# Low weight parts from ScalarE and an accumulating DMA instead of a VectorE subtraction, in a two-layer encoder trunk

## The chip, the cores and the metric

One core of one Trainium2 chip runs the whole program. The metric is the device time of one launch in microseconds. TensorE (PE) multiplies, VectorE (DVE) and ScalarE (ACT) work on 128 partitions, GpSimd (POOL) does a few small things, and SyncE (SP) issues the transfers from memory.

## The reference

Two layers of an encoder on 512 positions of width 1024, all in float32. A layer is a half-step feed-forward block (FFN), a mixer and a second half-step FFN:

```
h = x + 0.5 * swiglu(rms_norm(x, g1), w_gate, w_up, w_down)
z = rms_norm(h, g2) @ w_in            # u, v, xm, og
h = h + concat(spatial_gating(u, v), mlstm_mixer(xm, og)) @ w_out
x = h + 0.5 * swiglu(rms_norm(h, g3), w_gate, w_up, w_down)
```

The hidden width of an FFN is 2816. A final RMSNorm follows the second layer. Nearly all the arithmetic is in the products with the weights.

## The kernel before

Each product of float32 matrices is made of three matmuls on numbers that are rounded to a shorter format: weight and activation are each split into a high part (the rounded value) and a low part (the value less its high part), and high times high, high times low and low times high are added up in PSUM. A weight block is 128 x 1024 numbers (512 KB; 128 x 768 in the last down-projections of an FFN). One block is called a unit here, and a unit is used by 24 matmuls (18 for the small ones).

What a unit needs before PE can use it: an SP load into `raw` or `rawx`, an ACT copy into the high part `whi` or `whix`, and a DVE subtraction `raw - hi` into the low part `wlo` or `wlox`. Buffers set how far ahead this goes. `raw`, `whi` and `wlo` have three buffers each. Inside an FFN there are three more `rawx` and two more `whix` and `wlox`; the units of the gate and up product (the method `halves`) take `whix`/`wlox` and `whi`/`wlo` in turn. The down product and the mixer (the method `unit`) use `whi`/`wlo` alone. A unit's copy waits until PE is done with the unit that had the buffer.

The gate and up product of an FFN goes by pairs of hidden blocks, 43 pairs in all outside the very first, which is written out by hand. A pair has four weight blocks b11, b12, b22, b21 and uses seven units, e0 to e6 (`pair_plan`): e0, e3 and e5 are the plain blocks b11, b22 and b21; e1, e2, e4 and e6 are differences that `combine` makes on DVE in place. So e1 overwrites b11 with b12 - b11, and e6 overwrites b21. As seven is odd, the pairs alternate: in one e0 has the buffers `whi`/`wlo` and e3 and e5 have `whix`/`wlox`, in the next e0 has `whix`/`wlox`. On PE the seven units go into the PSUM banks pa, pe, pb, pe, pb, pa, pb in this order. An FFN has three groups of 4, 4 and 3 pairs, each followed by 8 down units; the last FFN of all runs its last 8 down units in two halves of the positions (`last_down`), with matmuls of half the width.

The program is put in order by a scheduler when it is built; on each engine the order is then fixed, and an instruction that waits holds up all that stand behind it. `load_params` makes small constants of the mixer on POOL at the start of each layer, from a transfer of parameters. POOL also adds up squares for the norms (`acc<-acc,sq`) and spreads rows in the mixer (`mb<-mr`).

Of the kernel before, what the change touches and what calls it, by code (L numbers as in the profile page):

```python
# [8 lines left out]
F32 = mybir.dt.float32  # L9
# [3 lines left out]
ALU = mybir.AluOpType  # L13
# [21 lines left out]
class Net:  # L35
# [77 lines left out]

    def unit(self, src, width=P):
        u = self.open_unit(src)
        self.fill(u, 0, u[0].shape[1])
        return self.views(u, width)

    def take(self):
# [12 lines left out]
        self.nc.sync.dma_start(out=raw, in_=src.rearrange("p j i c -> p (j i c)"))  # L132
        return raw

    def halves(self, raw):
        nc = self.nc
        self.wturn = getattr(self, "wturn", 0) + 1
        if self.wturn % 2:
            hi = self.phase.tile([P, 1024], F32R, tag="whix", name="whix", bufs=2)
            lo = self.phase.tile([P, 1024], F32R, tag="wlox", name="wlox", bufs=2)  # L140
        else:
            hi = self.wp.tile([P, 1024], F32R, tag="whi", name="whi")
            lo = self.wp.tile([P, 1024], F32R, tag="wlo", name="wlo")
        self.copied = nc.scalar.copy(hi, raw)  # L144
        nc.vector.tensor_tensor(out=lo, in0=raw, in1=hi.bitcast(F32), op=ALU.subtract)  # L145
        return tuple(t.rearrange("p (j i c) -> p j i c", j=4, i=2) for t in (hi, lo))

    def combine(self, out, a, c):
# [346 lines left out]
def pair_plan(blocks):  # L495
    st = {}

    def e0(b):
        st["b11"] = b.load(blocks[0])
        return b.halves(st["b11"])  # L500

    def e1(b):
        st["b12"] = b.load(blocks[1])
        b.combine(st["b11"], st["b12"], st["b11"])
        return b.halves(st["b11"])

    def e2(b):
        st["b22"] = b.load(blocks[2])
        b.combine(st["b11"], st["b22"], st["b11"])
        return b.halves(st["b11"])  # L510

    def e3(b):
        return b.halves(st["b22"])

    def e4(b):
        b.combine(st["b12"], st["b22"], st["b12"])
        return b.halves(st["b12"])

    def e5(b):
        st["b21"] = b.load(blocks[3])  # L520
        return b.halves(st["b21"])

    def e6(b):
        b.combine(st["b21"], st["b21"], st["b11"])
        return b.halves(st["b21"])

    return [e0, e1, e2, e3, e4, e5, e6]


# [631 lines left out]
```

## Time and profile before

| | |
|---|---|
| time, median of 3 runs | 1799.95 us (1799.25 to 1801.56) |
| time of the profiled execution | 1800.38 us |
| its span (first to last instruction) | 1798.7 us |
| PE busy | 1758.3 us (98%) |
| DVE busy | 1409.4 us (78%) |
| ACT busy | 880.4 us (49%) |
| POOL busy | 141.4 us (8%) |
| transfers from memory | 169.67 MB, the 16 DMA engines busy 31.0% of the span |
| granted TensorE clock, mean | 0.988 |

The profiled execution takes 1.7 us more than its span. Busy shares are means over stages that differ, so what an engine's relief is worth is read where PE waits.

### The profile page before, as it was taken

How to read it: one execution, taken by the hardware profiler on the slowest of the kernel's cores; microseconds unless marked ns; L12 is line 12 of the kernel's file. 1: busy time of each engine (PE TensorE's matmuls, PEld its weight loads, DVE VectorE, ACT ScalarE, POOL GpSimd, SP SyncE). 2: the span in 40 equal slices, each digit the busy share in tenths (PEclk: the TensorE clock that was granted, in tenths of full speed). 3: DMA queues.
4: the chain of work that ended last, by engine and by line, in shares of the span. 5: the costliest groups of instructions: out<-in, count | busy, mean ns of one | idle time of the engine just before them, and what ended most of it. 6: DMA issues, size and time to landing. Idle time of an engine off the chain costs nothing.

```text
span 1798.7 us, 28298 instructions
## 1 busy us (share of the span) xinstructions
PE 1758.3 (98%) x11602; PEld 1607.3 (89%) x11602; DVE 1409.4 (78%) x2062; ACT 880.4 (49%) x1233; POOL 141.4 (8%) x185
## 2 busy tenths in 40 slices
PE   8999999999998999999989999999999989999998
PEld 8989989887887989989889899898888889899898
DVE  8957958668988957958899587595698989597685
ACT  7434424457556534525565244344575555253255
POOL 5100000103012000000140000002030300000000
PEclk9999999999999999999999999999999989999999
DMA  5342422321241333323324233223122223233223
GB/s 187 94 130 94 128 73 80 99 80 50 69 140 48 110 125 94 119 82 100 99 69 141 83 94 122 91 73 105 59 60 83 94 83 126 86 105 118 83 77 109
DMA packets 51394, 173.60 MB, mean 97 GB/s; under 512 B 5824, under 2 KB 7872, under 8 KB 51264
## 3 DMA queue, kind: packets, MB, share of 16 engines
q1 hardware_dynamic: 51264, 171.79, 31.0%
q8 instruction: 91, 1.49, 0.3%
q14 instruction: 39, 0.32, 0.1%
HBM read 169.67 MB, written 2.10 MB: 95 GB/s over the span
## 4 chain that ended last, share of the span: by engine, by line
PE 83%; DVE 11%; ACT 3%; issue 2%; DMA 1%; SPq 0%; POOL 0%; DVEq 0%; ACTq 0%; POOLq 0%
PE pd L206 8%; PE pd L208 8%; PE pd L207 8%; PE pb L159 6%; PE pb L161 6%; PE pb L160 6%; PE pe L159 4%; PE pe L160 4%; PE pe L161 4%; PE pa L160 4%; PE pa L159 4%; PE pa L161 4%; PE pm L206 3%; PE pm L208 3%; PE pm L207 3%
## 5 line engine op out<-in xcount | busy, mean ns | idle before, releaser
L179 ACT CAST whi<-raw 128x1024 fp32r<-128x1024 f32 (+2 forms) x157 | 151.8, 967 | 310.5 <-PE pd L207 157.8
L207 PE MATMUL pd<-hl,whi 128*128 128x512 f32 (+1 forms) x752 | 282.6, 376 | 0.6 <-DVE hl L441 0.6
L208 PE MATMUL pd<-hh,wlo 128*128 128x512 f32 (+1 forms) x752 | 282.6, 376 | 0.5 <-DVE wlo L180 0.5
L206 PE MATMUL pd<-hh,whi 128*128 128x512 f32 (+1 forms) x752 | 282.9, 377 | 0.0
L180 DVE TENSOR_TENSOR wlo<-raw,whi 128x1024 fp32r<-128x1024 f32 (+2 forms) x157 | 176.2, 1123 | 29.1 <-ACT whi L179 28.0
L587 DVE SCALAR_TENSOR_TENSOR x<-pd,x 128x512 f32<-128x512 f32 x88 | 60.6, 689 | 149.9 <-PE pd L208 149.9
L144 ACT CAST whi<-rawx 128x1024 fp32r<-128x1024 f32 x86 | 88.7, 1048 | 160.9 <-DVE rawx L149 98.8
L206 PEld LDWEIGHTS pd<-hh,whi 128*128 128x128 f32 x752 | 141.4, 188 | 28.9 <-ACT hh L440 3.9
L208 PEld LDWEIGHTS pd<-hh,wlo 128*128 128x128 f32 x752 | 141.5, 188 | 26.2 <-DVE wlo L180 0.8
L207 PEld LDWEIGHTS pd<-hl,whi 128*128 128x128 f32 x752 | 141.6, 188 | 25.9 <-DVE hl L441 0.8
L159 PE MATMUL pb<-xh,whix 128*128 128x256 f32 x528 | 151.5, 287 | 3.5 <-ACT u L474 2.7
L161 PE MATMUL pb<-xh,wlox 128*128 128x256 f32 x528 | 151.2, 286 | 0.0
L160 PE MATMUL pb<-xl,whix 128*128 128x256 f32 x528 | 151.1, 286 | 0.0
L161 PE MATMUL pb<-xh,wlo 128*128 128x256 f32 x504 | 142.2, 282 | 0.5 <-DVE wlo L145 0.5
L159 PE MATMUL pb<-xh,whi 128*128 128x256 f32 x504 | 142.5, 283 | 0.0
L160 PE MATMUL pb<-xl,whi 128*128 128x256 f32 x504 | 142.5, 283 | 0.0
L144 ACT CAST whix<-rawx 128x1024 fp32r<-128x1024 f32 x86 | 89.7, 1049 | 107.1 <-PE pb L160 62.3
L145 DVE TENSOR_TENSOR wlox<-rawx,whix 128x1024 fp32r<-128x1024 f32 x86 | 105.8, 1231 | 8.7 <-ACT whix L144 8.7
L145 DVE TENSOR_TENSOR wlo<-rawx,whi 128x1024 fp32r<-128x1024 f32 x86 | 105.3, 1224 | 9.0 <-ACT whi L144 8.5
L144 ACT CAST whi<-raw 128x1024 fp32r<-128x1024 f32 x64 | 67.1, 1048 | 92.1 <-issue 37.3
L292 POOL TENSOR_TENSOR acc<-acc,sq 128x512 f32<-128x512 f32 x33 | 62.2, 1886 | 575.2 <-ACT sq L288 574.6
L159 PEld LDWEIGHTS pb<-xh,whix 128*128 128x128 f32 x528 | 102.7, 194 | 4.4 <-ACT u L474 2.9
(332 smaller groups left out, 5164.4 us busy)
## 6 DMA issues: line engine op xcount, KB each, us to landing
rawx<-in_wst SPq DMA_DIRECT2D x86, 512.0 KB, 3.6
raw<-in_wst SPq DMA_DIRECT2D x86, 512.0 KB, 3.7
raw<-in_wd SPq DMA_DIRECT2D x64, 512.0 KB, 3.7
raw<-in_wd SPq DMA_DIRECT2D x37, 384.0 KB, 3.1
raw<-in_win SPq DMA_DIRECT2D x24, 512.0 KB, 3.6
raw<-in_wo SPq DMA_DIRECT2D x16, 512.0 KB, 3.6
raw<-in_wv SPq DMA_DIRECT2D x8, 512.0 KB, 3.6
x<-in_xT SPq DMA_DIRECT2D x8, 256.0 KB, 4.7
```

The lines of the kernel that those rows point to most:

```text
L144: self.copied = nc.scalar.copy(hi, raw)
L145: nc.vector.tensor_tensor(out=lo, in0=raw, in1=hi.bitcast(F32), op=ALU.subtract)
L159: nc.tensor.matmul(o, whi[:, j, i, :], hi, start=f, stop=False, skip_group_check=True)
L160: nc.tensor.matmul(o, whi[:, j, i, :], lo, start=False, stop=False, skip_group_check=True)
L161: nc.tensor.matmul(o, wlo[:, j, i, :], hi, start=False, stop=j == 3, skip_group_check=True)
L179: self.copied = nc.scalar.copy(hi[:, r], raw[:, r])
L180: nc.vector.tensor_tensor(out=lo[:, r], in0=raw[:, r], in1=hi[:, r].bitcast(F32), op=ALU.subtract)
L206: nc.tensor.matmul(ps, whi[:, k0 + k, :], xh, start=k == 0, stop=False)
L207: nc.tensor.matmul(ps, whi[:, k0 + k, :], xl, start=False, stop=False)
L208: nc.tensor.matmul(ps, wlo[:, k0 + k, :], xh, start=False, stop=k == n - 1)
L292: self.added = (eng or nc.gpsimd).tensor_tensor(out=self.acc, in0=self.acc, in1=sq, op=ALU.add)
L587: nc.vector.scalar_tensor_tensor(out=xd, in0=pd, scalar=0.5, in1=xd, op0=ALU.mult, op1=ALU.add)
```

## The change

For every unit of `unit` and for e0, e3 and e5 of each pair, the low part is no longer subtracted on DVE. ACT copies the high part as before, ACT then writes its negative into the low part, and a DMA that POOL issues adds `raw` onto it in SBUF. There are 278 such DMAs. The region in which DMAs issued by POOL keep their descriptors grows from 1024 to 2048 bytes of each partition. The hand-written first pair and the differences e1, e2, e4 and e6 keep the subtraction.

```diff
     def unit(self, src, width=P):
         u = self.open_unit(src)
-        self.fill(u, 0, u[0].shape[1])
+        self.nc.sync.dma_start(out=u[1], in_=u[0])
+        self.lower(u[2], u[3], u[1])
         return self.views(u, width)
...
-    def halves(self, raw):
+    def lower(self, hi, lo, raw):
+        nc = self.nc
+        self.copied = nc.scalar.copy(hi, raw)
+        nc.scalar.mul(lo, hi.bitcast(F32), -1.0)
+        nc.gpsimd.dma_start(out=lo, in_=raw, accum_op=ALU.add)
+
+    def halves(self, raw, direct=False):
...
-        self.copied = nc.scalar.copy(hi, raw)
-        nc.vector.tensor_tensor(out=lo, in0=raw, in1=hi.bitcast(F32), op=ALU.subtract)
+        if direct:
+            self.lower(hi, lo, raw)
+        else:
+            self.copied = nc.scalar.copy(hi, raw)
+            nc.vector.tensor_tensor(out=lo, in0=raw, in1=hi.bitcast(F32), op=ALU.subtract)
...
-        return b.halves(st["b11"])
+        return b.halves(st["b11"], True)
...
-        return b.halves(st["b22"])
+        return b.halves(st["b22"], True)
...
-        return b.halves(st["b21"])
+        return b.halves(st["b21"], True)
...
-    nc = bacc.Bacc("TRN2", target_bir_lowering=False, num_devices=1, dynamic_dma_scratch_size=1024)
+    nc = bacc.Bacc("TRN2", target_bir_lowering=False, num_devices=1, dynamic_dma_scratch_size=2048)
```

The lines of the file move by one to ten: `combine` is line 149 before and 159 after, the subtraction of `halves` 145 and 155, the accumulating DMA is line 140, the negation line 139.

**Place 1, the start of the program on POOL.** Before, these rows are the end of `load_params` and then the first zeroing of tiles for the mixer:

```order
L647 TENSOR_TENSOR ct<-wqs,params 128x16
L649 TENSOR_TENSOR m_762<-m_762,ct 128x16
L663 TENSOR_TENSOR M<-bdmask,m_762 128x128 x4
L694 MEMSET xp 128x2
L695 MEMSET xp 128x2
```

Now the same place, where the first three DMAs are those of e0, e3 and e5 of the first pair that `pair_plan` makes:

```order
L657 TENSOR_TENSOR ct<-wqs,params 128x16
L659 TENSOR_TENSOR m_767<-m_767,ct 128x16
L673 TENSOR_TENSOR M<-bdmask,m_767 128x128 x4
L140 DMA wlox<-rawx 128x1024
L140 DMA wlo<-rawx 128x1024
L140 DMA wlo<-raw 128x1024
```

All accumulating DMAs stand on POOL's queue, and the first of them stands behind the whole of the first `load_params`.

**Place 2, the same stage on DVE.** Here `acc` are the sums of squares, `rstd`, `nt` and `nv` the norm, and `rawx_480` is b11 of that first pair. Before:

```order
L145 TENSOR_TENSOR wlox_483<-rawx_480,whix_482 128x1024 [waits DMAHW1_49,PE_49,Activation_49]
L292 TENSOR_TENSOR acc_92<-acc_92,sq_443 128x512 [waits DVE_49]
L149 TENSOR_TENSOR rawx_480<-raw_486,rawx_480 128x1024 [waits DMAHW2_49,DVE_49]
L292 TENSOR_TENSOR acc_92<-acc_92,sq_446 128x512 [waits DVE_49]
L149 TENSOR_TENSOR raw_486<-rawx_493,raw_486 128x1024 [waits DMAHW4_49,DVE_49]
```

Now (DMASW names the completion of a DMA that POOL issued):

```order
L336 TENSOR_SCALAR nv_454<-ss_452 128x512 [waits PE_49]
L340 RECIPROCAL rstd_456<-nt_455 128x512 [waits Activation_49]
L159 TENSOR_TENSOR rawx_480<-raw_487,rawx_480 128x1024 [waits DMAHW2_49,DMAHW1_49,DMASW0_49]
L232 TENSOR_TENSOR nt_455<-rstd_456 128x512 [waits DVE_49]
L159 TENSOR_TENSOR raw_487<-rawx_494,raw_487 128x1024 [waits DMAHW4_49,DVE_49]
L233 SCALAR_TENSOR_TENSOR nt_455<-nt_455,nv_454 128x512 [waits DVE_49]
L155 TENSOR_TENSOR wlo_491<-rawx_480,whi_490 128x1024 [waits Activation_49]
```

The combine that overwrites b11 now waits for the DMA that reads b11, and it stands ahead of the last steps of the norm.

**Place 3, a pair in the middle of an FFN whose e0 has the buffers `whix`/`wlox`, on DVE.** Before, from the subtraction of e0 on; `rawx_2083` is b11:

```order
L145 TENSOR_TENSOR wlox_2086<-rawx_2083,whix_2085 128x1024 [waits DMAHW2_49,Activation_49]
L149 TENSOR_TENSOR rawx_2083<-raw_2113,rawx_2083 128x1024 [waits DMAHW3_49,DVE_49]
L483 TENSOR_TENSOR U_2144<-pb_1987,e5_2077 128x512 [waits PE_49]
L149 TENSOR_TENSOR raw_2113<-rawx_2148,raw_2113 128x1024 [waits DMAHW4_49,DVE_49]
L145 TENSOR_TENSOR wlo_2117<-rawx_2083,whi_2116 128x1024 [waits Activation_49]
```

Now, with `rawx_2109` as b11:

```order
L159 TENSOR_TENSOR rawx_2109<-raw_2140,rawx_2109 128x1024 [waits DMAHW3_49,DMAHW2_49,DMASW2_49]
L498 TENSOR_TENSOR G_2172<-pa_2010,rstd_456 128x512 [waits PE_49]
L159 TENSOR_TENSOR raw_2140<-rawx_2175,raw_2140 128x1024 [waits DMAHW5_49,DVE_49]
L155 TENSOR_TENSOR wlo_2144<-rawx_2109,whi_2143 128x1024 [waits Activation_49]
L499 TENSOR_TENSOR G_2172<-pb_2012,rstd_456 128x512 [waits PE_49]
L159 TENSOR_TENSOR rawx_2109<-rawx_2175,rawx_2109 128x1024 [waits DVE_49]
L501 TENSOR_TENSOR G_2172<-G_2172,U_2171 128x1024 [waits Activation_49]
L155 TENSOR_TENSOR wlox_2179<-rawx_2109,whix_2178 128x1024 [waits Activation_49]
```

And ACT there, from the copy of e5 of the pair ahead, with `raw_2042` as b21 of the pair ahead:

```order
L138 CAST whix_2044<-raw_2042 128x1024 [waits DMAHW1_49,PE_49]
L482 COPY e5_2103<-pe_2011 128x512 [waits PE_49]
L139 ACTIVATE wlox_2045<-whix_2044 128x1024 [waits DMASW4_49,Activation_49]
L484 COPY u2_2104<-pb_2012 128x512 [waits DVE_49]
L138 CAST whix_2111<-rawx_2109 128x1024 [waits DMAHW2_49,PE_49]
L139 ACTIVATE wlox_2112<-whix_2111 128x1024 [waits DMASW0_49,PE_49,Activation_49]
L154 CAST whi_2074<-raw_2042 128x1024 [waits DVE_49]
L154 CAST whi_2143<-rawx_2109 128x1024 [waits DVE_49]
L138 CAST whi_2207<-rawx_2175 128x1024 [waits DMAHW5_49,PE_49]
```

The combine of e1 moved from right behind DVE's own subtraction to behind a DMA, and the readout of PSUM (`G<-pa`) now stands behind that combine.

## Rows read from the trace of the kernel before

**Rows 1.** First part of the page: busy us, share of the span, instructions.

```profile
PE 1758.3 (98%) x11602; PEld 1607.3 (89%) x11602; DVE 1409.4 (78%) x2062; ACT 880.4 (49%) x1233; POOL 141.4 (8%) x185
```

**Rows 2.** Two stretches, a pair and eight down units: busy us, PEclk, DMA.

```profile
187.65:207.60 19.95, 19.95 (x171) 19.95 (x170) 18.65 (x18) 10.92 (x13) 0.00 (x0) 1.00 0.35 106
247.50:289.90 42.40, 42.40 (x263) 38.31 (x262) 26.21 (x26) 13.97 (x15) 0.00 (x0) 1.00 0.29 87
```

**Rows 3.** Groups of ACT and DVE by form: count, busy us, mean ns.

```profile
L179 ACT CAST whi<-raw 128x1024 fp32r<-128x1024 f32 x112 | 117.6, 1050 | 260.1 <-PE pd L207 147.8 <-issue 39.1 <-PE pb L160 20.6
L490 ACT ACTIVATE G<-G 128x1024 f32<-128x1024 f32 x43 | 45.6, 1059 | 23.0 <-DVE G L489 22.9
L179 ACT CAST whi<-raw 128x768 fp32r<-128x768 f32 x37 | 30.9, 834 | 50.4 <-issue 14.9 <-PE pd L207 10.0 <-PE pa L160 9.7
L180 DVE TENSOR_TENSOR wlo<-raw,whi 128x1024 fp32r<-128x1024 f32 x112 | 137.5, 1229 | 25.8 <-ACT whi L179 25.2 <-ACT hh__4772 L912 0.3
```

**Rows 4.** DMA issues of the page: count, KB each, us to landing.

```profile
raw<-in_wd SPq DMA_DIRECT2D x64, 512.0 KB, 3.7
raw<-in_wd SPq DMA_DIRECT2D x37, 384.0 KB, 3.1
```

**Rows 5.** POOL at the start: start us, us, what, idle before.

```profile
24.62 4.05 POOL L647 TENSOR_TENSOR rc<-params 128x64 f32<-128x64 f32 x1 [20.05 <-DMA params<-in_params]
36.38 1.29 POOL L649 TENSOR_TENSOR rc<-rc,ct 128x64 f32<-128x64 f32 x1
40.41 0.30 POOL L647 TENSOR_TENSOR ct<-params 128x64 f32<-128x64 f32 x1
50.55 1.47 POOL L663 TENSOR_TENSOR M<-bdmask,m 128x128 f32<-128x128 f32 x4
```

**Rows 6.** PE and ACT in that stage.

```profile
32.41 0.28 PE L161 MATMUL pa<-xh,wlox 128*128 128x256 f32 x1
55.23 0.58 ACT L474 COPY u<-pb 128x512 f32<-128x512 f32 x1
55.86 0.39 PE L159 MATMUL pb<-xh,whix 128*128 128x256 f32 x1 [2.70 <-ACT u L474]
```

**Rows 7.** The stretch behind that wait: busy us, PEclk (0.50).

```profile
56.41:59.82 3.41, 3.41 (x18) 3.41 (x17) 3.41 (x4) 0.00 (x0) 0.00 (x0) 0.50 0.55 156
```

**Rows 8.** POOL and PE where the second layer starts.

```profile
926.03 0.65 POOL L649 TENSOR_TENSOR rc<-rc,ct 128x64 f32<-128x64 f32 x1
925.85 0.39 PE L161 MATMUL pa<-xh,wlox 128*128 128x256 f32 x1 [0.85 <-DVE wlox L145]
```

**Rows 9.** PE, ACT and DVE around two pairs.

```profile
187.65 0.28 PE L159 MATMUL pa<-xh,whi 128*128 128x256 f32 x1
207.58 0.28 PE L159 MATMUL pa<-xh,whix 128*128 128x256 f32 x1
188.00 1.04 ACT L144 CAST whix<-rawx 128x1024 fp32r<-128x1024 f32 x1
199.18 1.05 ACT L144 CAST whix<-rawx 128x1024 fp32r<-128x1024 f32 x1 [0.56 <-ACT u L474]
201.52 1.23 DVE L149 TENSOR_TENSOR rawx<-raw,rawx 128x1024 f32<-128x1024 f32 x1
202.66 0.68 DVE L483 TENSOR_TENSOR U<-pb,e 128x512 f32<-128x512 f32 x1
```

**Rows 10.** Spacing of units: ACT in a down stage and in `last_down`.

```profile
249.49 1.06 ACT L179 CAST whi<-raw 128x1024 fp32r<-128x1024 f32 x1 [4.34 <-PE pd L207]
254.93 1.05 ACT L179 CAST whi<-raw 128x1024 fp32r<-128x1024 f32 x1 [4.38 <-PE pd L207]
1785.94 0.42 ACT L391 ACTIVATE sq<-x 128x256 f32<-128x256 f32 x1 [1.14 <-DVE x L607]
1788.10 0.42 ACT L391 ACTIVATE sq<-x 128x256 f32<-128x256 f32 x1 [1.34 <-DVE x L607]
```

**Rows 11.** The stage between the first mixer and its FFN: busy us.

```profile
540.00:562.00 22.00, 13.87 (x80) 11.38 (x79) 20.68 (x25) 12.91 (x19) 10.90 (x4) 0.91 0.16 49
```

## The prediction

> **What bounds the kernel now.** I read the page's busy shares first: PE is busy in 1758.3 us of its span of 1798.7, 98% [rows 1]. So 40.4 us is the most that a relief of any other engine could give. Then I read two stretches with the engines side by side: in a pair PE is busy 19.95 of 19.95 us beside 18.65 of DVE and 10.92 of ACT; in eight down units 42.40 of 42.40 beside 26.21 of DVE [rows 2]. The reader is to see that DVE is near the limit inside a pair, but that PE is the bound in both. A unit of a pair is 19.95 / 7 = 2.85 us, one of a down stage 42.40 / 8 = 5.3 us. The question is therefore not what DVE gains, but whether each low part still comes before PE wants it.
>
> **What is removed and added.** Of the 278 low parts 241 are 1024 wide and 37 are 768 wide; 129 belong to pairs (3 x 43) and 149 to `unit` (112 + 37). DVE loses 241 x 1.229 us and 37 subtractions of some 0.9 us, together 330 us. ACT gains 241 negations at 1.06 us (the ACTIVATE of 128x1024) and 37 at 0.83, together 286 us: with 880 us before it comes to 1166 of 1799, 65%, not a bound as a mean [rows 3]. What matters is the delay. Before, a low part came 1.23 us after its copy; now it comes 1.06 us (the negation) and one accumulating DMA after it. I call A the time from POOL's issue of that DMA to its landing.
>
> **The unknown, A.** No accumulating DMA, and none from SBUF to SBUF, is in the trace of before. The nearest row is a load of the same 512 KB: 3.7 us from issue to landing; 384 KB takes 3.1 [rows 4]. So 128 KB more costs 0.6 us, and one stream of 512 KB some 2.4 us besides a fixed part of 1.3. Lower bound: the second stream (the destination has to be read too) is hidden, A = 3.7. Middle: it is paid in full, 3.7 + 2.4 = 6.1 (384 KB: 3.1 + 1.8 = 4.9). Upper bound: the DMA also shares the 16 engines with one load, another 2.4, and POOL's issue is slowed beside DVE as its small instructions are (1.29 us for one beside DVE, 0.30 for one of the same size when DVE is quieter [rows 5]), another 1.0: A = 9.5. I take 6.1, since both streams must pass through the same 16 engines and nothing in the rows makes the second free.
>
> The page "DMA: Bandwidth & Descriptors" of the Trainium skill, section "Anatomy of one DMA — SWDGE (gpsimd) path", has a fixed cost of about 2 us for a DMA issued by GpSimd, most of it the receipt of the last write. With the page's rate that makes an estimate of some 4.4 us for two streams; the sum below would then be about 30 instead of 83 us. No run here shows it yet.
>
> **Term 1, the start: +11 us.** POOL waits for the parameters and then runs `load_params` from 24.62 to 52.02 us, one instruction behind the other, slowed while DVE is busy [rows 5]. The first accumulating DMA stands behind all of it (place 1). As DVE has less to do now, I let the later 31 instructions go at about 0.35 us: the DMA goes out at about 44.5, lands at 50.6. PE used this low part at 32.41 [rows 6], and it waits for it now. Worse, DVE's combine of e1 waits for the same DMA at the head of DVE's queue (place 2), and behind it stand nine instructions 1024 wide (counted at 1.23 as in [rows 3]) and seven 512 wide (half of that) up to the readout of PSUM by ACT, itself 0.58: 50.6 + 16 = 66.6 us at the end of the copy that PE then waits for, which ended at 55.81 before [rows 6]. That is 11 us; 8.6 at A = 3.7, 14.4 at A = 9.5. After such a wait the granted clock was 0.50, that is 1.2 GHz, for 3.41 us with 18 matmuls [rows 7], which at the full clock take half, so a wait of this kind costs 1.7 us more; I count that only where I say so, as before has this one already.
>
> **Term 2, the second layer's start: +7.7 us.** There the last steps of `load_params` are on POOL until 926.7, while PE wants the first low parts at 925.85 [rows 8]. The DMA behind it lands at 926.7 + 6.1 = 932.8, 6.9 us late, and the combine of e6, which waits for e5's DMA, adds 0.8. At A = 3.7 it is 5.3, at 9.5 it is 11.1.
>
> **Term 3, the pairs: +51 us.** Two pairs that follow each other stand for all [rows 9]. In the pair whose e0 has `whix` PE starts at 207.58. The buffer is free for its copy at 199.18; copy and negation end at 201.3, the DMA lands at 207.4, and the low part is wanted two matmuls behind the start (171 in 19.95 us are 0.12 apart [rows 2]), at 207.82: just hidden. But e1's combine (1.22 us; before, it started at 201.52) now waits until 207.4. Behind it stand a readout (0.68), the next combine and e1's subtraction, 1.22 each (place 3): e1's low part is there at 211.7, and PE wants it at 210.67. It is 1.0 late. Up to e2's low part DVE has 0.68 + 3 x 1.22 = 4.34 us to do, where PE uses 2.85: 1.5 more. Together 2.5 us. In the other kind of pair (start 187.65) e3 is the narrow place: copy at 188.00, another cast, the negation, DMA out at 191.1, landing at 197.2; e3 is wanted at 187.65 + 3 x 2.85 + 0.24 = 196.4, so 0.8 late. The mean is 1.65. I count it for the 31 of the 43 pairs that are not the first of their group; ahead of the others eight down units give the lead. 31 x 1.65 = 51. At A = 3.7 both kinds lie hidden (0.1 late at most); at 9.5 they are 5.9 and 4.2 late, 155 us, and the 12 first pairs may add 2 each, 24.
>
> **Term 4, the down units and mixers: +17 us.** In a down stage the copies of units are 5.44 us apart [rows 10], and three buffers let a copy start two units ahead: 10.9 us, against 1.06 + 1.06 + 6.1 = 8.2. These are hidden, up to A of about 9. A unit of 768 has 18 matmuls, 4.0 us by the same pace: 8 us against 0.83 + 0.83 + 4.9 = 6.6, hidden too. Where the cover is gone is `last_down`: its units are 2.16 apart [rows 10], so the lead is 4.3 + 0.24 = 4.6 against 6.6, 2.0 late; I take four such waits in it, each with 1.2 us of low clock, 13 us (1 at A = 3.7, 24 at 9.5). For mixers and small units where ACT, now with a third more work, comes behind, I add 4 (0 and 15).
>
> **Term 5, DVE's relief: -4 us.** Between the first mixer and its FFN DVE is busy 20.68 of 22.00 us and PE only 13.87 [rows 11]; there a subtraction taken away may move PE forward. About five of 1.2 us stand there, and both layers and the second half have such a place: at most 3 x 6 = 18 us. Since the first low parts of the FFN now come by POOL and wait, I take 4.
>
> **Sum.** 11 + 7.7 + 51 + 13 + 4 - 4 = 83 us. The profiled execution took 1800.38 us, 1.7 more than its span and 0.4 above the median of the runs, so the time is 1800.4 + 83 = 1883 us; the 0.4 is below what the sum can tell.
>
> **Rivals.**
> *The DMA is short.* A is 3.7 to 4.5: the second stream costs little. For it speaks that the engines are only 29 to 35% busy in the stretches shown [rows 2]; against it, that one stream's share is read from two rows alone. At 3.7: 8.6 + 5.3 + 1 - 4 = +11, 1811 us. At 4.5 the `whix` pairs are 0.9 late (31 x 0.45 = 14), the start 9.4, the second layer 6.1, `last_down` 7: +32, 1833 us. It is this time that the page's fixed cost above would give.
> *The DMA is long.* A = 9.5 by the upper bound: 14.4 + 11.1 + 155 + 24 + 24 + 15 - 4 = +239, 2040 us. For it speaks that POOL's work is slowed beside DVE, that three DMAs of a pair and its loads share 16 engines, and that one waiting DMA on POOL holds all behind it.
> *Not slower.* The DMA is short and DVE's relief is had in full at the three transitions: 18 us of gain against 15 of the two starts, about 1798. It decides only from A below 4, and if POOL ends `load_params` as early as I let it. For it speaks the idle PE there; against it that the combine at the head of DVE's queue now waits in the same stages.
> That the subtractions stay on DVE somewhere is excluded by the order of DVE's instructions.
>
> **Numbers.** A measurement of this kernel tells about 0.2% (3.6 us) from no change. Forecast, A from 4.6 to 8 (1840 to 1935 us): 0.50. Short DMA (1805 to 1840): 0.20. Long (above 1935, to 2060): 0.24. Not slower: 0.06, of it 0.03 faster, and 0.01 more for a gain that I do not see. The predicted time is 1883. The range leaves out the not slower case and half of the long one and so holds some 8 in 10: 1808 to 1995. Faster 0.04, the same 0.03, slower 0.93.
>
> **What would show it.** Right: POOL's first DMA at 44 to 47 us and a wait of PE of about 18 us for a `wlox` there; waits of DVE's combine for a DMA; in pairs waits of PE for `wlo` or `wlox`, in a sum of some 50 us, more in those whose e0 has `whix`; waits in `last_down` for DMAs. The table of DMA issues gives A itself for the 512 KB form. Wrong, if A is under 4.6 or over 8, if PE stands in down stages (A above 9), if POOL's issue and not the landing is the delay, or if ACT, whose queue has two instructions more for each low part's path, holds the readouts of PSUM.

## The result, and the profile after

The changed kernel takes 2042.6 us (median of 4 runs, 2037.3 to 2043.9) against 1799.6: a ratio of 1.134, interval 1.132 to 1.136. It is 243 us slower; the forecast was 83 slower, with a range up to 1995. The profiled span is 2042.0 us, so before and after can be compared span by span.

First parts of the page (they answer to [rows 1]), then its DMA queues with packets, bytes and their share of 16 engines' span, and the DMA issues with their median time to landing ([rows 4]):

```profile
PE 1830.0 (90%) x11602; PEld 1649.1 (81%) x11602; DVE 1107.3 (54%) x1784; ACT 1140.4 (56%) x1515; POOL 351.0 (17%) x463
...
q0 software_dynamic: 40032, 140.92, 37.1%
q1 hardware_dynamic: 51264, 171.79, 26.9%
...
wlo<-raw POOLq DMA_DIRECT2D x134, 512.0 KB, 5.9
rawx<-in_wst SPq DMA_DIRECT2D x86, 512.0 KB, 4.0
...
raw<-in_wd SPq DMA_DIRECT2D x64, 512.0 KB, 5.1
wlox<-rawx POOLq DMA_DIRECT2D x43, 512.0 KB, 4.7
...
wlox<-raw POOLq DMA_DIRECT2D x21, 512.0 KB, 6.2
```

DVE is relieved by 302 us (330 forecast), and nothing comes of it. PE's busy time grew by 72 us though it does the same 11602 matmuls, and its idle time from 40 to 212 us: 172 + 72 is the whole loss. Of the idle time 108 us end with the landing of a DMA (none before), 69 with DVE (13 before) and 26 with ACT (16). Of the busy part some 39 us are the clock: TensorE's granted clock is 0.50 (1.2 GHz) in 30 stretches of 147 us in all, before in 9 of 44 us, and each lies in or close behind waits of PE. There a matmul 256 wide takes 224 ns of PE's busy time, elsewhere 124 (before 120). The other 33 us are such small differences at the full clock, and no run explains them. The accumulating DMAs take 37% of the engines for 141 MB, the loads 27% for 172 MB, so a byte of them costs 1.7 times the engine time of a byte loaded. Over all 278, A is 3.9 to 10.4 us, 5.9 in the mean, 5.4 in the median. They seldom wait on POOL: an issue starts 0.44 us behind the end of its negation in the mean, and three of the 278 over 1 us behind it.

Both programs have PE's matmuls in stages of the same number, so the stages can be set beside each other, from the start of a stage to the start of the next. Gate and up stages are 152.6 us longer in sum, down stages 61.2 (22 of it in the last one, 23 with the norm's ends), mixers with the head of the program and these ends 29.0.

PE's longest waits, and DVE's for DMAs (us in total, times, longest), in the changed kernel:

```profile
PE pd L218 <- DMA wlo<-raw: 33.2, 17, 3.7
PE pb L169 <- DVE U L493: 29.3, 17, 2.6
PE pa L171 <- DMA wlo<-raw: 24.9, 13, 2.8
PE pa L171 <- DMA wlox<-raw: 20.6, 12, 6.6
PE pa L171 <- DMA wlox<-rawx: 16.2, 4, 11.7
...
DVE raw L159 <- DMA wlo<-raw: 108.3, 22, 7.9
DVE raw L159 <- DMA wlox<-raw: 65.8, 21, 5.4
DVE rawx L159 <- DMA wlo<-rawx: 55.4, 12, 8.4
...
DVE rawx L159 <- DMA wlox<-rawx: 24.7, 7, 7.2
```

In a pair, pa with a low part from `raw` is e5. `DVE raw L159` is e6's combine, which overwrites b21 and so waits for e5's DMA to have read it: in each of the 43 pairs, 174 us in all. `DVE rawx L159` is e1's combine, which waits for e0's DMA, 80 us in all. `DVE U L493` is the readout of pb, which stands on DVE behind such a combine.

One pair, about its e5, from the timeline (start us, us, what, idle before). ACT, POOL, SP, DVE and PE rows follow each other:

```profile
192.23 1.05 ACT L138 CAST whi<-raw 128x1024 fp32r<-128x1024 f32 x1
...
197.92 1.06 ACT L139 ACTIVATE wlo<-whi 128x1024 fp32r<-128x1024 f32 x1
...
199.34 0.89 POOL L140 DMA_DIRECT2D wlo<-raw  x1 [3.75 <-ACT wlo L139]
202.32 0.87 POOL L140 DMA_DIRECT2D wlo<-rawx  x1 [2.09 <-ACT wlo L139]
...
199.28 0.33 SPq L133 DMA_DIRECT2D rawx<-in_wst  x1
199.70 0.38 SPq L133 DMA_DIRECT2D raw<-in_wst  x1
...
207.88 1.23 DVE L159 TENSOR_TENSOR raw<-raw,rawx 128x1024 f32<-128x1024 f32 x1 [6.54 <-DMA wlo<-raw]
...
211.37 1.22 DVE L159 TENSOR_TENSOR rawx<-raw,rawx 128x1024 f32<-128x1024 f32 x1
212.51 0.68 DVE L493 TENSOR_TENSOR U<-pb,e 128x512 f32<-128x512 f32 x1
...
207.91 0.39 PE L171 MATMUL pa<-xh,wlo 128*128 128x256 f32 x1 [1.44 <-DMA wlo<-raw]
213.34 0.35 PE L169 MATMUL pb<-xh,whix 128*128 128x256 f32 x1 [2.56 <-DVE U L493]
```

e5's copy is done at 193.28, but its negation stands on ACT behind five other instructions until 197.92. e5's DMA goes out at 199.34 together with two loads, the next pair's e0 follows at 202.32, and e5's takes 8.5 us. PE waits 1.44 us for it, DVE 6.54. The combine of the next pair's e1 (211.37) then stands ahead of the readout of pb, and PE waits another 2.56 us. All that the forecast said of a combine that waits for a DMA is here, but at e5, and the forecast had not priced e5. The negation is 4.6 us behind its copy in 14 of the 43 pairs; in the others mostly 0.4 us or less. e5's DMA takes 6.8 us in the mean.

### The profile page after: what moved, and what is told of

The parts are those of the page before. It is cut to its first block, busy times and chain, and to the rows that moved or that the text cites. A ratio compares the mean times of both kernels' runs of the same rounds, so it can differ in the third digit from the quotient of the medians.

```text
span 2042.0 us, 29332 instructions
## 1 busy us (share of the span) xinstructions
PE 1830.0 (90%) x11602; PEld 1649.1 (81%) x11602; DVE 1107.3 (54%) x1784; ACT 1140.4 (56%) x1515; POOL 351.0 (17%) x463
## 4 chain that ended last, share of the span: by engine, by line
PE 29%; issue 28%; DMA 24%; DVE 9%; ACT 7%; POOL 3%; SPq 0%; POOLq 0%; DVEq 0%; ACTq 0%
DMA wlo<-raw 13%; PE pd L218 3%; DMA raw<-in_wd 3%; PE pd L216 3%; PE pd L217 3%; DMA wlo<-rawx 2%; PE pm L218 2%; PE pm L217 2%; PE pm L216 2%; DMA wlox<-rawx 2%; DVE raw L159 2%; ACT whi L138 1%; DMA wlox<-raw 1%; DVE rawx L159 1%; ACT wlo L139 1%
## 5 line engine op out<-in xcount | busy, mean ns | idle before, releaser
L138 ACT CAST whi<-raw 128x1024 fp32r<-128x1024 f32 (+1 forms) x171 | 170.4, 1001 | 277.0 <-PE pd L217 170.0
L218 PE MATMUL pd<-hh,wlo 128*128 128x512 f32 (+1 forms) x752 | 290.8, 388 | 33.2 <-DMA wlo<-raw 33.2
L216 PE MATMUL pd<-hh,whi 128*128 128x512 f32 (+1 forms) x752 | 288.5, 385 | 8.3 <-ACT hh L450 6.1
L140 POOL DMA_DIRECT2D wlo<-raw x171 | 148.3, 869 | 751.8 <-ACT wlo L139 609.8
L139 ACT ACTIVATE wlo<-whi 128x1024 fp32r<-128x1024 f32 (+1 forms) x214 | 217.3, 1020 | 3.6
L169 PE MATMUL pb<-xh,whix 128*128 128x256 f32 x528 | 156.5, 296 | 30.1 <-DVE U L493 29.3
L171 PE MATMUL pb<-xh,wlox 128*128 128x256 f32 x528 | 155.4, 294 | 11.4 <-DVE wlox L155 11.4
L159 DVE TENSOR_TENSOR raw<-raw,rawx 128x1024 f32<-128x1024 f32 x43 | 52.7, 1226 | 174.0 <-DMA wlo<-raw 108.3
L171 PE MATMUL pa<-xh,wlox 128*128 128x256 f32 x344 | 102.6, 298 | 36.9 <-DMA wlox<-raw 20.6
L171 PE MATMUL pa<-xh,wlo 128*128 128x256 f32 x344 | 102.5, 298 | 27.1 <-DMA wlo<-raw 24.9
L171 PEld LDWEIGHTS pb<-xh,wlox 128*128 128x128 f32 x528 | 105.7, 200 | 14.3 <-DVE wlox L155 14.3
L159 DVE TENSOR_TENSOR rawx<-raw,rawx 128x1024 f32<-128x1024 f32 x43 | 52.6, 1222 | 115.8 <-DMA wlo<-rawx 55.4
```

Source lines behind the costliest of these rows:

```text
L139: nc.scalar.mul(lo, hi.bitcast(F32), -1.0)
L140: nc.gpsimd.dma_start(out=lo, in_=raw, accum_op=ALU.add)
L159: self.nc.vector.tensor_tensor(out=out, in0=a, in1=c, op=ALU.subtract)
L169: nc.tensor.matmul(o, whi[:, j, i, :], hi, start=f, stop=False, skip_group_check=True)
L171: nc.tensor.matmul(o, wlo[:, j, i, :], hi, start=False, stop=j == 3, skip_group_check=True)
L216: nc.tensor.matmul(ps, whi[:, k0 + k, :], xh, start=k == 0, stop=False)
```

## The experiments

Two theories stood against each other. **S (sharing)**: alone the DMA is shorter than assumed, but in company of loads and other DMAs twice as long, just where it matters. **L (plain latency)**: it has about one A everywhere, and there was less slack than assumed. Beside them: ACT's negations, or DVE's queue. Where no interval is given, a time is one run, beside 1797.8 to 1802.3 of the kernel before.

**The DMA by itself.** Six times each, behind one gate (a small operation on DVE that all of them wait for):

```
nc.gpsimd.dma_start(out=t["lo1"], in_=t["src1"], accum_op=ALU.add)   # alone; or with
nc.sync.dma_start(out=t["in1"], in_=src[0])                          # one or two loads
```

> A kernel that only moves data: it measures the time from issue to landing of the accumulating DMA alone, of half and a quarter of it, of plain copies and of loads, and of mixtures, each started together, six times; it computes nothing of the reference. Theory S (sharing): the DMA alone takes about 4.4 us (the shortest of the changed kernel's are 3.9 to 4.6) and 7 us or more beside two loads, 8.5 or more for the second of two beside two loads. Theory L (plain latency): it takes about 5.9 us, the mean in the changed kernel, alone, and at most 1 us more in company.

By line (count, then times to landing): alone (L32), a plain copy in SBUF by POOL (L41), beside two loads (L60), the second of two (L64), the second of two beside two loads (L70).

```profile
L32 POOL DMA_DIRECT2D big<-big x6: 862/862/1005, 6.3 to 31.7; - x6
DMA to landing us min/median/max: 4.5/4.5/4.6
...
L41 POOL DMA_DIRECT2D big<-big x6: 530/530/557, 79.7 to 97.1; - x6
DMA to landing us min/median/max: 2.8/2.9/2.9
...
L60 POOL DMA_DIRECT2D big<-big x6: 856/862/872, 209.1 to 252.9; - x6
DMA to landing us min/median/max: 7.8/8.1/8.3
...
L64 POOL DMA_DIRECT2D big<-big x6: 1205/1214/1240, 261.8 to 300.5; - x6
DMA to landing us min/median/max: 6.6/6.6/6.7
...
L70 POOL DMA_DIRECT2D big<-big x6: 1130/1214/1232, 308.3 to 364.6; - x6
DMA to landing us min/median/max: 9.8/10.1/10.2
```

A is 4.5 us alone, 3.3 at half the columns and 2.7 at a quarter, 8.1 beside two loads, 10.1 at worst. S holds for the DMA by itself: company nearly doubles it, and the pair above (8.5) has that company. An estimate of 4.4 us for two streams was worked out ahead of the result from the page "DMA: Bandwidth & Descriptors" of the Trainium skill, section "Anatomy of one DMA — SWDGE (gpsimd) path". The lone DMA agrees with it; the kernel's mean of 5.9 does not, as the estimate knows no company.

**Which DMAs.** Units alone, pairs alone, and each plain block of the pairs alone:

```diff
-        return b.halves(st["b11"], True)
+        return b.halves(st["b11"])
```

> Only the 149 units of the down product and the mixer get the DMA; the pairs keep the subtraction on DVE. If the stages' losses add up by themselves, the down stages (61 us longer in the changed kernel, 22 of it in the last one) and the mixers (29) are lost again: about 1885 us. If the DMAs of down units are only late because they meet those of pairs and what pairs delay (S), the last down stage loses its 22 and the rest less than half: 1835 to 1860 us.

> Only e0, e3 and e5 of the pairs get the DMA (129 of them). If losses add up, the 153 us of the gate and up stages come back and nothing else: about 1950 us. Under S a little less than that, 1930, since the first units of a down stage no longer put DMAs beside the last ones of a pair. If ACT's negations of the down units were what holds the pairs, under 1900 us.

> Only e0 of the pairs gets the DMA (43). If lost time comes in the places where a DMA stands in company and a combine waits behind it (S), e0 has the two starts of the layers, about 25 us, and part of the pairs: 1840 to 1860 us. If DMAs only hurt by being many on the engines, a third of the 189 us: 1860 us, no nearer told apart by this run alone.

> Only e3 gets the DMA (43). Nothing overwrites its raw block, and its DMAs took 4.7 us in the mean where only pairs had them. S with the waits of the combines: 1800 to 1815 us. If it is the number of DMAs, or ACT, a third of the 189 us: 1860 us. My own prediction had e3 as the narrow place of every second pair (0.8 us late at 6.1 us).

> Only e5 gets the DMA (43). Its DMA went out beside the loads of the next pair and took 6.8 us in the mean, and e6's combine waits for it at the head of DVE's queue. Without the DMAs of e0 and e3 in its company it is shorter, some 5.5 to 6 us. S: the largest part of the pairs' loss, 1850 to 1890 us. If the company of e0's DMA is needed for the loss, under 1830 us.

| DMAs at | time, us | against before | gate and up | of it, later groups | down | mixers |
|---|---|---|---|---|---|---|
| units (149) | 1854.3 | +56 | -10.5 | 0 | +31.6 | +32.2 |
| pairs (129) | 1987.8 | +189 | +175.1 | +102 | +8.2 | +4.1 |
| e0 (43) | 1884.3 | +82 | +79.7 | +45 | +0.2 | +4.0 |
| e3 (43) | 1809.8 | +8 | +9.7 | 0 | -0.2 | -0.1 |
| e5 (43) | 1856.5 | +54 | +52.3 | +16 | +3.8 | -0.1 |
| e3, e5 (86) | 1923.7 | +126 | +120.5 | +73 | +2.9 | -0.1 |
| all (278) | 2042.6 | +243 | +152.6 | +98 | +61.2 | +29.0 |

The stages are set against the profiled run of the kernel before, the times against runs beside them. The later groups are the second and third group of each FFN, 28 of the 43 pairs; the rest of a gate and up stage's loss lies in the first group of an FFN.

56 + 189 is 245: in total units and pairs add up. By stages they don't. The down stages lose 61 us in the whole change, 32 and 8 in the two runs, while the others lose less together. So pairs and units do make each other late where a down stage follows pairs: in four down stages of the changed kernel PE waits 3.3 to 3.6 us for the low part of the second unit, and the run with units alone has no such wait. Its 1854.3 lies in the range that S gave; that the mixers lose as much without the pairs speaks against S. The 1987.8 of the pairs is above all three figures given for it.

Inside the pairs they don't add up either: 8 + 54 + 82 is 144, and together they cost 189; e3 and e5 cost 126 instead of 62. In the later groups the three make 62 by themselves and 102 together. e3, which the forecast called the narrow place of every second pair, costs 8 us, nearly all at the very start. e0 was dearer than expected, 82 for 40 to 60. Of e5's price two thirds come in the first groups; alone its DMA takes 5.0 us in the mean and its negation mostly follows its copy at once, so the long way of the pair shown above comes only with the other DMAs.

**ACT's part.** The negation as in the change, then an addition on DVE in place of the DMA:

```diff
-        nc.gpsimd.dma_start(out=lo, in_=raw, accum_op=ALU.add)
+        nc.vector.tensor_tensor(out=lo, in0=raw, in1=lo.bitcast(F32), op=ALU.add)
```

> As the changed kernel, with ACT's negation, but the low part is then made by an addition on DVE in the place of the DMA; the result is the same. It has ACT's whole extra work and 1.06 us more delay, and no DMA. Theories S and L (the DMA's time is the loss): within 15 us of the time before, 1800 to 1815 us. The rival that ACT's longer queue holds the readouts: 1850 us or more.

1822.0 us, +23, above the 15 expected and far below the rival's 50. ACT's extra work and the longer way through its queue are a tenth of the loss. In this run no negation of a pair's e5 stands 4.6 us behind its copy, so that part of ACT's order in the changed kernel is not measured by it.

**The traffic alone**, on the kernel before:

```diff
+        self.nc.gpsimd.dma_start(out=t[:, :hi.shape[1]], in_=hi)   # twice, to memory
```

> The kernel before with its subtractions on DVE, but at each of the 278 places GpSimd also issues two plain writes of the high part to memory (2 x 512 KB, or 2 x 384), which nothing waits for but the next owner of the high part's buffer. The engines of the DMA are then about as busy as in the changed kernel, and no low part comes by DMA. If the lost time is the loads' (delayed by company), 1880 us or more. If it is the wait for the low parts themselves, within 20 us of before: 1800 to 1820 us.

1817.6 us, +18, with 44% of the engines' time in these writes, more than the 37% above, and `raw<-in_wd` loads at 6.6 us. So loads that come later cost little in the order of before, which leaves the waiting for the low parts.

**Half the bytes.**

```diff
-        nc.gpsimd.dma_start(out=lo, in_=raw, accum_op=ALU.add)
+        nc.gpsimd.dma_start(out=lo[:, :n], in_=raw[:, :n], accum_op=ALU.add)   # n: half the columns
```

> As the changed kernel, but the DMA adds only the first half of each block's columns (256 or 192 KB); the other half of a low part stays the negated high part. All waits are as they were. Alone this DMA takes 3.3 us instead of 4.5. If the loss follows the bytes that share the engines (S), a mean of some 4 us and two thirds of the loss back: 1850 to 1900 us. If it is a fixed delay and the waits as such, 1.2 us per DMA less, at most a third back: above 1960 us.

1956.5 us, with a mean A of 4.2. 86 of the 243 us come back, nearer to L's third than to S's two thirds: at a mean A below that of a lone whole DMA, 157 us are still lost. By stages it is two answers. The gate and up stages gave back 34 of their 153 us, the later groups 14 of 98, so there the length of the DMA is the small part. Down stages and mixers gave back 52 of 90, so there it is the larger.

**The starts and the last down stage** with the subtraction kept in the first pair planned in each layer and in the last down units:

> As the changed kernel, but the first pair that each layer plans and all units of the last down stage keep the subtraction on DVE. It measures my terms 1, 2 and 4. The first gate and up stage, 18.8 us longer than before in the changed kernel, should lose 10 to 13 of that, that of the second layer (14.3 longer) some 8, the last down stage all its 22: about 2000 us. If the start is bound by something else than the first DMA behind load_params, only the 22 come back: 2020 us.

2011.9 us, -31. The last down stage is as before again (-23). The first gate and up stage gave back 4.1 us, the second layer's 2.6, not the 10 to 13 and 8 expected. The first pair no longer waits for POOL, but the next pair's e0 does:

```profile
49.80 1.47 POOL L676 TENSOR_TENSOR M<-bdmask,m 128x128 f32<-128x128 f32 x4
51.21 1.00 POOL L143 DMA_DIRECT2D wlo<-rawx  x1
```

`load_params` ends some 10 us later in this run than in the changed kernel, and the first DMA stands right behind it again, 6.9 us behind the end of its negation. It lands at 56.81, and PE waits 4.5 us for it. So the place behind `load_params` was handed to another DMA; no run took it away.

**DVE's queue.** First e6's wait alone is taken away from the whole change:

```diff
-        b.combine(st["b21"], st["b21"], st["b11"])
-        return b.halves(st["b21"])
+        b.combine(st["b11"], st["b21"], st["b11"])
+        return b.halves(st["b11"])
```

> As the changed kernel, but e6's difference is written into the buffer of b11, which is free of readers by then, so that its combine no longer waits for e5's DMA to have read b21; the result is the same. If DVE's queue is what the wait costs (174 us of DVE's waits for this DMA, 29 us of PE's waits for a readout behind it), 40 to 80 us come back: 1965 to 2000 us. If PE only waits for e5's own low part, under 15 us come back: above 2028 us.

2057.4 us, 15 slower. DVE's waits there (the same view as above):

```profile
DVE rawx L159 <- DMA wlo<-rawx: 103.4, 19, 8.8
DVE rawx L159 <- DMA wlox<-rawx: 64.0, 17, 7.5
```

The 174 us at e6's combine are gone, and those at e1's combine, for e0's DMA, grew from 80 to 167. One wait took in part the place of the other, so this run couldn't tell. Hence five more: e1's combine behind the readout of pb, without and with e6's edit; and e3 and e5 alone, without and with e6's edit, where e0 has no DMA.

```diff
+                with b.tc.issue_after(b.read.ins):     # b.read: the readout of pb of the pair ahead
+                    b.combine(st["b11"], st["b12"], st["b11"])
```

> As the kernel with DMAs in the pairs alone (1987.8 us), but e1's combine is put behind the readout of pb of the pair ahead on DVE; before, every second pair had it ahead, and PE waited 29 us in all for that readout. If DVE's queue is the loss: 1930 to 1960 us. If the low parts are late by themselves, PE waits for them instead: 1975 to 2000 us.

> The same, and e6's difference goes into the buffer of b11, so that neither combine waits for a DMA ahead of a readout. If DVE's queue is the loss, below 1900 us. If the low parts are late by themselves: above 1950 us.

> Only e3 and e5 of the pairs get the DMA (86). Alone they cost 8 and 54 us: 1860 us if that adds up, 1880 or more if the company of their DMAs counts. Together with the run of e0 alone (+82) it tells how much of the 189 us is due to the three being together.

> The same with e6's difference in the buffer of b11: no combine waits for a DMA any more. If DVE's wait is e5's price: 1805 to 1830 us. If e5's own low part is late: as much as without it, 1855 us or more.

> As the changed kernel, with e1's combine behind the readout of pb and e6's difference in the buffer of b11, so that both waits at the head of DVE's queue are taken away. If one wait only took the place of the other in the run that took away e6's alone, some 70 us come back: 1960 to 1985 us. If DVE's queue doesn't count once the units have DMAs too: above 2025 us.

| | without | e1 behind the readout | and e6 in b11 |
|---|---|---|---|
| pairs | 1987.8 | 1938.2 | 1919.1 |
| e3, e5 | 1923.7 | | 1859.1 (e6's edit alone) |
| the whole change | 2042.6 | | 1991.4 |

DVE's queue is at least 50 to 69 us of the pairs' 189, half of the 126 of e3 and e5, and at least 51 of the whole 243: a real part, less than its theory asked (1900 and 1830). How it costs is plainest with e3 and e5. There PE's longest wait is this one:

```profile
PE pb L168 <- ACT u L483: 42.2, 19, 3.3
```

In one pair e6's combine waits for e5's DMA until 239.66, DVE's addition in pb stands behind it (240.80), ACT's copy of u comes behind that (241.94), and PE waits 2.61 us for the copy. With e6's edit no combine waits for a low part, this wait is gone from the view, and of the 73 us of the later groups 25 are left. "At least" stands for the other two rows because e1's combine still waits for e0's DMA there. In the whole change with both edits DVE waits 145 us at it (first two lines), and PE waits as follows:

```profile
DVE rawx L162 <- DMA wlox<-rawx: 78.3, 17, 7.5
DVE rawx L162 <- DMA wlo<-rawx: 66.3, 18, 8.7
...
PE pa L174 <- DMA wlox<-rawx: 19.2, 8, 11.9
PE pa L174 <- DMA wlox<-raw: 17.4, 8, 10.3
PE pd L221 <- DMA wlo<-raw: 17.4, 12, 4.5
PE pe L172 <- ACT e L485: 13.9, 16, 1.9
PE pb L174 <- DVE wlox L158: 13.5, 15, 1.0
```

The readout of pb (29.3 us in the changed kernel) is gone from the first places; what is left are the low parts that come by DMA, ACT's readouts, and low parts that DVE makes late (`DVE wlox L158`).

**More raw buffers in the last down stage**, six in place of three:

> As the changed kernel, with three more raw buffers in the last down stage alone (six in place of three); high and low parts keep their three buffers. If the loads are what comes late there, because a raw buffer is free only when its DMA has landed, the stage's 23 us (13.8 in the first half, 8.4 in the second) fall to 10 or less: about 2029 us. If the low parts' own way (copy, negation, DMA) is the limit, as the forecast had it, 13 or more of it stays and the time is above 2033 us; the table by stage decides, since the rest of the kernel varies by some us.

2032.1 us; the stage with its ends still loses 18.9 of its 23. A raw buffer held by the DMA is a small part. That leaves the low parts' own way through three high and three low buffers, as forecast; more of those were not tried.

**The places where a relief of DVE showed.** With units alone the gate and up stages were 10.5 us shorter. The DMA in 16 units:

```diff
+            yield one(wd6[d] if nk == 6 else wd8[gi, d], P, not (first and gi == 0 or before and gi == 2))
```

> Only the eight down units of the first group of all and the eight small ones ahead of the second layer get the DMA (16 of 278): the places where the run with units alone was shorter than before, 2.3 us in the first gate and up stage and 4.9 in that of the second layer, against 0.4 and 2.6 longer in the down stages themselves. If these gains are DVE's relief in the neighbouring stage: about 1795 us, 0.2% faster. If they came by the order of other work, no change, 1798 to 1802 us.

1796.7 us (12 runs), a ratio of 0.9984, interval 0.9976 to 0.9993: 2.6 us faster by the medians, and the only version that is faster than before. The second layer's first gate and up stage is 5.7 us shorter and the small down stage ahead of it 2.6 longer. That fits DVE's relief; a better order on DVE that came with it would look the same.

## Why the prediction was wrong

The sign, the bound (PE, nothing to gain from DVE in the pairs) and the kinds of waits were right. The size was not: 83 of 243.

- **A.** 6.1 was taken; the mean is 5.9. The number was right, as a mean. Wrong was that one number stood for all places: alone 4.5, in company 8 to 10. The bound of 9.5 was built of a collision with a load, which is there, and of a slowed issue on POOL, which is not: the issue took 0.86 us in the bench with DVE quiet and 0.87 in the changed kernel. So the rival "long DMA" came to 2040 with a uniform A of 9.5 that the kernel does not have; that it met the time is chance.
- **Term 1 (+11).** The first DMA went out at 41.09 (44.5 forecast) and landed at 45.6; PE's wait was 11.7 us, not 18, and 400 matmuls into the program PE is 12.7 us behind. ACT's copy ended at 66.5, forecast as 66.6 from a landing 5 us later than it was, so the size was right partly by chance.
- **Term 2 (+7.7).** PE waits 6.6 us there (6.9 forecast), for a DMA that went out right behind the last step of `load_params`; the stage as a whole is 14.3 longer, with three more pairs in it.
- **Term 3 (+51) is the step that failed.** Gate and up stages lost 152.6 us, about 130 without the two starts. The step priced a lone DMA at two narrow places, e0 with e1 behind it and e3, and found them hidden up to A = 3.7. It didn't price e5, whose low part and whose combine come late (16 us in the later groups when alone, and the longest waits of DVE). It took each lateness once, though one wait at the head of DVE's queue makes the readouts, ACT's copies and the next combine late: by themselves the three cost 62 us in the later groups, together 102. And it left out the low clock behind a wait. For the later groups it comes to 33 us (20 pairs at 1.65), and the whole change lost 98 there. Nor does the loss follow A as the step has it: at A = 4.2 the later groups still lose 84, where it would have had some 6. The other third of the loss is in the first groups of the FFNs, where it counted nothing for a group's first pair and terms 1 and 2 stand beside it.
- **The clock**, put at nothing outside `last_down`, is some 39 us of the 243. [rows 7] was also misread: its 18 matmuls take 2.1 us at the pace of [rows 2], so that stretch cost 1.3 us more, not 1.7.
- **Term 4 (+17).** The last down stage lost 23, not 13: PE waits six times for low parts there, 11.4 us in all where four waits of 2.0 were forecast, and the granted clock is 0.87 in it. The stages called hidden were not: the other down stages lost 39 us, the mixers 28, together 67 for the 4 taken. With units alone it is 11 and 31, so the down stages' part comes largely from the pairs ahead of them. Of the 14.4 and 13.2 us that the two mixers lose, 8.7 and 9.7 come behind the 840th of their 928 matmuls, in the products just ahead of the next FFN; why was not tried.
- **Term 5 (-4).** A gain exists: 10.5 us with units alone, 2.6 net where it is used alone.

The parts shown overlap and so don't add up: ACT's longer way 23, traffic on the engines 18 at most in the order of before, the queue of DVE at least 51, the last down stage 23; half the bytes are worth 86. That the rest is the low parts' own lateness is what PE's waits say (108 us for DMAs); no run took it away whole, and its cause in the pairs stays open in part.

## What to carry to other kernels

A transfer takes the time that it has in the company its own trigger brings: what frees it also frees loads, and here that nearly doubles it. What it costs depends on what stands behind it: in the down stages and mixers half the bytes gave back more than half of the loss, in the later groups of pairs a seventh. Where an operation with a fixed place on an engine becomes a chain over three queues, go through every use of it, not the narrowest two, and look at what stands between its links on each queue. And a transfer that reads a buffer in place turns each later overwrite into a wait at the head of the overwriting engine's queue; taking away one such wait may only show the next.

## What was not expected of the hardware

An accumulating DMA inside SBUF of 512 KB took 4.5 us where a plain copy took 2.9 and a load alone 3.2, and POOL needed 0.86 us to issue it, 0.53 for the copy. Two issued together took 4.6 and 6.6 us, and beside two loads 8.1 and 10.1: the later one is the one that company makes longer.
